# A hybrid diffusion block on one core: the router in a written order, the modulation product in four column groups, retention heads behind the last column blocks, the overflow branch moved, the last expert pair in full precision

## The chip, the core and the metric

The kernel runs on one core of a Trainium2 chip. The metric is the device time of one execution in microseconds (us). One core has a tensor engine (PE, with its weight loads shown apart as PEld), a vector engine (DVE), a scalar engine (ACT), GpSimd (POOL) and SyncE (SP), which here issues nearly all transfers. Each engine runs its own instructions in the order in which they stand in its queue.

## What is computed

One layer on 256 latent tokens and 256 context tokens of width 2048, all in fp32. Cut to what matters (plain_norm, silu and softmax as usual; S = 256, D = 2048):

```python
mod_x = split(silu(c) @ w_ada + b_ada, 6)          # six vectors of 2048 for the latent tokens
mod_c = split(silu(c_ctx) @ w_ada + b_ada, 6)      # the same for the context tokens
lat = modulate(x, mod_x[0], mod_x[1]) @ w_in       # 2048 -> qr kr vr gr (1024 each), cq 512, ckv 256, kpe 64
con = modulate(ctx, mod_c[0], mod_c[1]) @ w_in
s_fwd, s_bwd = context_retention_states(kr_c, vr_c)              # 8 heads of 128
ret = silu(gr) * plain_norm(bidirectional_retention(axial_rope(qr), axial_rope(kr), vr, s_fwd, s_bwd)) * gn_w
att = block_attention(mla_queries(cq), mla_keys_values(context and latent ckv, kpe))   # 8 heads
h = layer_norm(ALPHA * x + mod_x[2] * (concat(ret, att) @ w_o), ln1)
t = modulate(h, mod_x[3], mod_x[4])
g = argmax(t @ w_group + b_group)                                 # one of 4 groups
top2 = top_k((t @ w_route + b_route)[g], 2)                       # two of its 8 experts, weighted
y = sum over the 32 experts of gate * ((silu(t @ w_gate) * (t @ w_up)) @ w_down)       # 2048 -> 512 -> 2048
out = layer_norm(ALPHA * h + mod_x[5] * y, ln2)
```

## The kernel before, in words

The program is one straight line of stages. A scheduler that plans with its own costs places instructions of different statements between one another on each engine; what it decides is read from the order of the instructions.

**Modulation and input projection.** Of the six modulation vectors the first two (shift and scale ahead of the projection) are needed at once. gemv_plan makes them on TensorE: silu(c) and silu(c_ctx) are the stationary operand, a block of 128 rows by 32 columns, and the weights stream through. The block uses only 32 columns of the array, so the kernel has two 32-column groups run beside each other: a piece holds the columns of one of the two vectors (m) for some rows, and its even and odd row blocks go to the groups 2m and 2m+1 (L526). Weights come through `st`, four buffers of 1 MB that everything ahead of the experts streams through. The projection itself is done in six stages over blocks of 128 input rows: STAGES = 1, 1, 2, 4, 4 and 4 blocks. Within a stage the loop runs over chunks of w_in (a 1 MB chunk of four rows by 512 columns in the last three, ten chunks per stage, ci), loads one, splits it into a rounded part on ACT (L273) and a rest on DVE (L274), and multiplies three times (L594 to L596). Chunks that serve both streams fill four PSUM banks, those for latent tokens alone two. The modulation of stage k+1 is made during stage k: the loop hands out `todo`, the pieces of gemv_plan, over the chunks.

**The other four vectors** (m = 2 to 5) are made by ada_steps: one step takes 1 MB of w_ada, scaled and added up by two DVE instructions (L250) or by POOL. ADA_V says how many DVE steps stand behind which chunk, ADA_V_MLA behind each attention head. ada_finish (L210) brings the vectors 3 and 4 into a column form by 16 matmuls of one column (L215).

**Retention** runs in the last projection stage (stage 5). Behind chunk 3 the rotation of k goes to POOL (rope, L312 to L317), behind chunk 5 that of q to DVE, followed by all eight heads (ret_tables, ret_head: products with the context, scores L393, the mask on DVE L396 and L397, the result L402 and L404, L406 and L407 its statistics). Four chunks are left behind them: gates, cq and ckv/kpe.

**Attention, output projection, router.** The attention heads come next, then the output projection (L852 to L854) in four blocks n of 512 columns. Each block's end adds into h (L871, L872, statistics L873). The router's logits are computed from unnormalized h (router_part per half block, transposes L169, squares, L834 and L835) and corrected by mean and variance with many instructions of a few columns (L893 to L912), followed by maxima and one-hots (L944 to L954). The norm itself is `affine` (L181, L182), two DVE instructions per 128x512 piece, eight pieces; behind it each piece is normed again on ACT and split into a rounded part and a rest (nn). The counts of the selected tokens (L957 to L961) give each token its place, then tokens are gathered per expert by one-hot matmuls (L1049).

**Experts.** 32 experts in 16 pairs, 64 slots each. Every expert takes six chunks of 2 MB through a ring of six buffers, 192 chunks in all: gate and up (L1071), down (L1116). The result is scaled by the gate into a rounded part D (ACT, L1122) and a rest (DVE, L1123), and two matmuls per block (scatter, L1130) add it to the tokens, scaled by vector 5 and added to h (L1131, L1132). Gathering for the next two pairs happens between the down chunks of every odd pair. Only in pair 5 it doesn't: there overflow() (L1134 to L1138), a branch on whether an expert has more than 64 tokens, stands behind the downs and scatters, and eight gather steps stand behind it. The last pair's down chunks are ordered so that norm_part can make the final statistics block by block.

## Time and profile before

| what | value |
|---|---|
| median of three runs | 1685.78 us (1684.48 to 1687.98) |
| the profiled execution | 1686.18 us, of which its span is 1684.4 us |
| PE busy | 1521.6 us, 90% of the span |
| DVE, ACT, POOL busy | 919.9, 484.2, 105.9 us |
| read from memory | 575.81 MB; 343 GB/s over the span, written bytes included |

How to read it: shares over the whole span mix stages with different limits. The page gives the span in 40 slices of 42 us; a table by windows gives the busy time of every engine in each stage. In it, "(x231)" is a count of instructions, PEclk the granted clock as a share of full speed, and the last two columns are the DMA engines' busy share and what they moved. Where one line serves many places, groups are read by line and window.

### The profile page before, as it was taken

The page shows a single profiled execution, that of the slowest core. Times are in us where ns is not written, and L with a number is a line of the kernel's source. Part 1 is how long each engine was busy: PE and PEld are TensorE (multiplying, and loading weights), DVE is VectorE, ACT ScalarE, POOL GpSimd, SP SyncE. Part 2 cuts the span into 40 slices and gives each one's busy share as a digit, 9 for nine tenths or more (in the row PEclk, how much of TensorE's full clock was granted, in tenths as well). Part 3 has the DMA queues.
Part 4 walks back from the last instruction along what each step waited for, and adds up shares of the span by engine and source line. Part 5 has one row for each costly group of instructions (what it writes and reads, how often), then busy time and mean ns, then how long its engine had stood idle before and what let it go on. Part 6 is the DMA issues. An engine that isn't in the chain of part 4 may idle for free. (4 is left out here: it accounts for less than half of the span.)

```text
span 1684.4 us, 20454 instructions
## 1 busy us (share of the span) xinstructions
PE 1521.6 (90%) x8316; PEld 919.2 (55%) x8316; DVE 919.9 (55%) x1553; ACT 484.2 (29%) x913; POOL 105.9 (6%) x91
## 2 busy tenths in 40 slices
...
PEclk8999999998999999899999999999999999999997
...
GB/s 326 272 326 283 294 309 286 276 245 225 184 192 153 199 270 360 225 301 426 426 427 427 426 427 425 370 428 427 427 427 427 427 426 427 426 426 427 421 425 136
DMA packets 54226, 579.28 MB, mean 344 GB/s; under 512 B 6320, under 2 KB 6768, under 8 KB 8816
## 3 DMA queue, kind: packets, MB, share of 16 engines
...
q0 software_dynamic: 128, 0.03, 0.0%
HBM read 575.81 MB, written 2.10 MB: 343 GB/s over the span
## 5 line engine op out<-in xcount | busy, mean ns | idle before, releaser
L1071 PE MATMUL pA<-we,xg 128*64 128x512 f32 x2048 | 468.0, 602 | 12.8 <-DMA we<-in_wexp_dram 12.8
L1071 PEld LDWEIGHTS pA<-we,xg 128*64 128x64 f32 x2048 | 140.8, 138 | 281.2 <-issue 247.6
L1116 PE MATMUL pA<-we,hT 128*64 128x256 f32 x2048 | 232.7, 382 | 17.4 <-DMA we<-in_wexp_dram 16.1
L1123 DVE SCALAR_TENSOR_TENSOR D<-pA,gcol,D 64x256 fp32r<-64x256 f32 x256 | 123.5, 482 | 176.0 <-ACT D L1122 175.3
L273 ACT CAST whi<-st 128x1024 fp32r<-128x1024 f32 (+3 forms) x130 | 125.1, 965 | 282.5 <-PE pA L596 172.5
L1116 PEld LDWEIGHTS pA<-we,hT 128*64 128x64 f32 x2048 | 147.4, 137 | 92.2 <-ACT D L1122 8.7
L595 PE MATMUL pA<-wlo,xhi 128*128 128x512 f32 (+1 forms) x480 | 188.2, 392 | 10.5 <-DVE wlo L274 10.5
L594 PE MATMUL pA<-whi,xhi 128*128 128x512 f32 (+1 forms) x480 | 185.5, 394 | 3.3 <-ACT whi L273 3.1
L596 PE MATMUL pA<-whi,xlo 128*128 128x512 f32 (+1 forms) x480 | 185.8, 387 | 0.0
L250 DVE SCALAR_TENSOR_TENSOR ada_acc<-st,c,ada_acc 128x1024 f32<-128x1024 f32 x128 | 177.5, 1406 | 8.3 <-DMA st<-in_ada_dram 8.2
L274 DVE TENSOR_TENSOR wlo<-st,whi 128x1024 fp32r<-128x1024 f32 (+2 forms) x122 | 134.6, 1112 | 57.6 <-ACT whi L273 57.1
L1122 ACT ACTIVATE D<-pA,gcol 64x256 fp32r<-64x256 f32 x256 | 120.0, 469 | 156.7 <-PE pA L1116 87.5
L1074 ACT ACTIVATE hid<-pA 128x256 f32<-128x256 f32 x32 | 12.3, 383 | 493.5 <-PE pA L1071 493.5
L1075 DVE TENSOR_TENSOR hid<-pA,hid 128x256 f32<-128x256 f32 x32 | 13.5, 423 | 219.7 <-ACT hid L1074 219.7
L594 PEld LDWEIGHTS pA<-whi,xhi 128*128 128x128 f32 x480 | 90.5, 191 | 37.5 <-ACT whi L273 17.7
L595 PEld LDWEIGHTS pA<-wlo,xhi 128*128 128x128 f32 x480 | 91.9, 191 | 31.9 <-DVE wlo L274 14.5
L1058 DVE TENSOR_SCALAR xg<-pT,modt 128x256 f32<-128x256 f32 x64 | 34.8, 544 | 131.2 <-PE pA L1071 93.7
L1131 DVE TENSOR_TENSOR pA<-pA,ada_acc 128x512 f32<-128x512 f32 x128 | 83.5, 693 | 36.8 <-PE pA L1130 36.6
L596 PEld LDWEIGHTS pA<-whi,xlo 128*128 128x128 f32 x480 | 92.0, 192 | 16.3
L1049 PE MATMUL pT<-oh,nn 128*128 128x256 f32 x512 | 80.5, 303 | 9.1 <-DVEq L1136 5.8
L1049 PEld LDWEIGHTS pT<-oh,nn 128*128 128x128 f32 x512 | 68.3, 199 | 31.7 <-issue 20.5
L1132 DVE TENSOR_TENSOR h<-pA,h 128x512 f32<-128x512 f32 x128 | 82.6, 683 | 0.8
...
## 6 DMA issues: line engine op xcount, KB each, us to landing
we<-in_wexp_dram SPq DMA_DIRECT2D x190, 2048.0 KB, 21.8
...
```

What stands on the lines that cost most here:

```text
L250: V.scalar_tensor_tensor(accs[m][:, sl], w[:, sl], c2[:, k, 0:1], accs[m][:, sl], op0=OP.mult, op1=OP.add)
L273: A.copy(hi, src)
L274: (eng or V).tensor_tensor(lo, src, hi, op=OP.subtract)
L594: T.matmul(banks[t][:, :wd], xh[:, sl], hi[:, kk, :wd], start=fst, stop=False)
L595: T.matmul(banks[t][:, :wd], xh[:, sl], lo[:, kk, :wd], start=False, stop=False)
L596: T.matmul(banks[t][:, :wd], xl[:, sl], hi[:, kk, :wd], start=False, stop=lst)
L1049: T.matmul(p[:, 256 * j:256 * j + width], nnh[i % 2][:, i // 2, ks], oh[:, i // 2, :width], start=(i == 0), stop=(i == 3))
L1071: T.matmul(pg[64 * cg:64 * cg + 64], xg[:, k, c0:c0 + 64], c[:, kk, 512 * cg:512 * cg + 512], start=(k == 0), stop=(k == KB - 1))
L1116: T.matmul(pd[64 * cg:64 * cg + 64, :256], hT[:, f % 2, 64 * (f // 2):64 * (f // 2) + 64], c[:, f, 256 * cg:256 * cg + 256], start=(f == 0 ...
L1122: A.activation(hl[0][rows, sl], p, AF.Copy, scale=g)
L1123: V.scalar_tensor_tensor(hl[1][rows, sl], p, g, hl[0][rows, sl], op0=OP.mult, op1=OP.subtract)
L1131: V.tensor_tensor(p, p, mod5[:, sl], op=OP.mult)
```

## The change

Eight edits, in the order of the program:

1. **gemv pieces**: a piece now loads both vectors' columns, and for each row block runs m = 0 and m = 1 behind one another, so that four column groups are in use. GEMV_AT says behind which chunks of the ten-chunk stages the pieces stand. The order on PE of the start is written out (manual_schedule).
2. **Order of column blocks** in stages 1 to 4: blocks for both streams and blocks for latent tokens alone alternate.
3. **ada_finish**: four matmuls of 512 columns in four column groups, an ACT copy and four transposes in place of 16 matmuls of one column. **ada steps**: the sequence of DVE steps begins earlier (23 instead of 20 in stages 0 to 4, 10 instead of 14 in stage 5), attention has 17 instead of 14, and two steps of vector 5 fewer run in the output projection.
4. **Retention**: rope of k on DVE; heads 0 and 1 behind chunk 6, two more behind each of chunks 7, 8 and 9; a head's tables are made two heads ahead.
5. **router_consts**: four reductions, 1.4 us each, at four places of the output projection instead of one.
6. **Router**: from the last block on, the order of DVE, ACT and PE is written out. Of the eight norm instructions of each kind (L181 and L182 before, L913 and L917 after) three and two stand ahead of the selection, where square roots are awaited; the others stand behind it, in turn with the rests of nn. Small instructions of the two token tiles alternate.
7. **Overflow**: the branch stands behind gate and up of pair 5, ahead of its downs, and pair 5 gathers like the other odd pairs.
8. **Last pair**: D stays in fp32, the L1123 instructions fall away there, and the scatter is one fp32 matmul in place of two.

The places where instructions move, from the written order of the instructions. Names: pG is a bank of gemv_plan, pA a bank of a product, st a stream buffer, whi/wlo and xhi/xlo the rounded parts and rests of weights and inputs, lv, AM, Ssb and xq the values, masked scores, states and scaled queries of a retention head, qk its transposed queries and keys, ct the constants.

PE in stage 3, at one gemv piece, before:

```order
L594 MATMUL pA<-whi,xhi 128x512
L595 MATMUL pA<-wlo,xhi 128x512
L596 MATMUL pA<-whi,xlo 128x512
L526 MATMUL pG<-st,csil 32x512 x4
L594 MATMUL pA<-whi,xhi 128x512 x2
```

The same engine and stage after:

```order
L604 MATMUL pA<-wlo,xhi 128x512
L605 MATMUL pA<-whi,xlo 128x512
L535 MATMUL pG<-st,csil 32x512 x8
L603 MATMUL pA<-whi,xhi 128x512
L604 MATMUL pA<-wlo,xhi 128x512
```

Two pieces of four, 25 rows apart in the former order, have become one of eight; at some places of stages 3 and 4 it is split into one and seven.

PE in stage 5, from the middle of one retention head into the next, before:

```order
L402 MATMUL pA<-lv,AM 128x128
L404 MATMUL pA<-Ssb,xq 128x128 x2
L402 MATMUL pA<-lv,AM 128x128 x2
L404 MATMUL pA<-Ssb,xq 128x128 x2
L381 MATMUL pA<-vz,ck 128x256
L393 MATMUL pA<-qk 128x256 x2
L169 MATMUL pT<-ct,lq 128x128
L169 MATMUL pT<-ct,lk 128x128 x2
```

The same engine after, where a head ends behind which projection stands:

```order
L409 MATMUL pA<-lv,AM 128x128
L411 MATMUL pA<-Ssb,xq 128x128 x2
L409 MATMUL pA<-lv,AM 128x128 x2
L411 MATMUL pA<-Ssb,xq 128x128 x2
L604 MATMUL pA<-wlo,xhi 128x512
L605 MATMUL pA<-whi,xlo 128x512
L603 MATMUL pA<-whi,xhi 128x512
L604 MATMUL pA<-wlo,xhi 128x512
```

Between two pairs of heads now stand 20 to 24 projection matmuls; before, only the heads' own work stood there.

DVE in the router, from the correction of the logits to the first maxima, before:

```order
L182 SCALAR_TENSOR_TENSOR h<-h,hs,D_5453 128x512
L190 RECIPROCAL hs<-hs 128x2
L181 SCALAR_TENSOR_TENSOR h<-h,hs,D_5452 128x512
L909 TENSOR_TENSOR hs<-hs 128x2
L912 SCALAR_TENSOR_TENSOR L<-L,hs,rc 128x40 x2
L944 MAX gm<-L 128x8
L182 SCALAR_TENSOR_TENSOR h<-h,hs,D_5453 128x512
L945 MAX_INDEX gi<-gm,L 128x8
L944 MAX gm<-L 128x8
L181 SCALAR_TENSOR_TENSOR h<-h,hs,D_5452 128x512
```

The same engine after:

```order
L913 SCALAR_TENSOR_TENSOR h<-h,hs,D_5445 128x512
L957 RECIPROCAL hs<-hs 128x2
L958 TENSOR_TENSOR hs<-hs 128x2
L960 SCALAR_TENSOR_TENSOR L<-L,hs,rc 128x40 x2
L993 MAX gm<-L 128x8 x2
L994 MAX_INDEX gi<-gm,L 128x8
L1049 TENSOR_SCALAR w<-gm 128x1
L994 MAX_INDEX gi<-gm,L 128x8
L995 CAST gf<-gi 128x8
```

The 128x512 norm instructions that stood among the small ones are gone from there, but for the first.

The diff, cut to its core:

```diff
-ADA_V = [[0] * 10, [0] * 10, [0] * 5, [1] * 10, [1] * 10, [2] * 4 + [1] * 6]
+ADA_V = [[0] * 3, [1, 0, 0], [1, 1, 1, 0, 1], [1] * 7 + [0, 1, 1], [1] * 7 + [0, 1, 1], [1] * 10]
+
+GEMV_AT = (1, 3, 4, 5, 6)
...
         order = [2, 3, 4, 5, 0, 1, 9, 8, 6, 7]
+    elif si:
+        order = [0, 2, 1, 3, 6, 4, 7, 8, 5, 9]
     else:
...
-    ada_v = [(m, k) for m in (3, 4, 2) for k in range(KB)]
-    ada_g = [(5, k) for k in range(KB)]
+    ada_g = [(m, k) for m in (3, 4, 2, 5) for k in range(KB)]
+    ada_v = [ada_g.pop(0) for _ in range(50)]
...
             p = bankT()
-            for k in range(KB):
-                T.matmul(p[:, k:k + 1], acc[:, 128 * k:128 * k + 128], ones[:, 0:1], start=True, stop=True)
-            if m == 4:
-                V.tensor_scalar(modt[:, 1], p[:, :KB], 1.0, None, op0=OP.add)
-            else:
-                V.tensor_copy(modt[:, 0], p[:, :KB])
+            for g in range(4):
+                T.matmul(p[32 * g:32 * g + 32], ones[:, 0:32], acc[:, 512 * g:512 * g + 512], start=True, stop=True)
+            row = sa.tile([128, 2048], F32, name="st", tag="st")[:, :512]
+            A.copy(row, p)
+            p = bankT()
+            for j in range(4):
+                transpose(p[:, 128 * j:128 * j + 128], row[:, 128 * j:128 * j + 128])
+            V.tensor_scalar(modt[:, m - 3].rearrange("p (g j) -> p g j", g=4),
+                            p.rearrange("p (j g r) -> p g j r", j=4, g=4)[:, :, :, 0], float(m - 3), None, op0=OP.add)
...
-        def piece(j, m):
+        def piece(j):
...
-                c = stream(dram2(a["ada01"], base + (m * nch + j) * 128 * per * w, 128, per * w), per * w)
+                c = [stream(dram2(a["ada01"], base + (m * nch + j) * 128 * per * w, 128, per * w), per * w)
+                     for m in range(2)]
                 for kk in range(per):
                     k = j * per + kk
-                    g = 2 * m + (k % 2)
-                    T.matmul(p[32 * g:32 * g + 32, :w], csil[:, k], c[:, kk * w:kk * w + w],
-                             start=(k < 2), stop=(k >= KB - 2))
+                    for m in range(2):
+                        g = 2 * m + (k % 2)
+                        T.matmul(p[32 * g:32 * g + 32, :w], csil[:, k], c[m][:, kk * w:kk * w + w],
+                                 start=(k < 2), stop=(k >= KB - 2))
...
         for j in range(nch):
-            pieces.append(piece(j, 0))
-            pieces.append(piece(j, 1))
+            pieces.append(piece(j))
...
+            if nchunk == 10:
+                n = GEMV_AT.count(ci)
...
-                            rope(pl["k"][:, t, 512 * j:512 * j + 512], t, "ck", "sk", 4, 64, R["rt"], G)
+                            rope(pl["k"][:, t, 512 * j:512 * j + 512], t, "ck", "sk", 4, 64, R["rt"])
                 elif ci == 5:
                     for t in range(2):
                         for j in range(2):
                             rope(pl["q"][:, t, 512 * j:512 * j + 512], t, "cq", "sq", 4, 64, R["rt"])
-                    for h in range(H):
+                    for h in range(2):
                         ret_tables(h)
+                if ci > 5:
+                    for h in range(2 * ci - 12, 2 * ci - 10):
                         ret_head(h)
-                elif ci == LAT:
+                        if h < H - 2:
+                            ret_tables(h + 2)
...
-    ada_steps(48, 0)
+    ada_steps(len(ada_v), 0)
...
-        for i, v in enumerate((pr[0], pr[2], pr[1], wrm)):
-            V.tensor_reduce(rc[:, i], v.rearrange("p k n -> p n k"), axis=AX.X, op=OP.add)
-        return bias
+        return bias, (pr[0], pr[2], pr[1], wrm)
+
+    def router_const(i, v):
+        V.tensor_reduce(rc[:, i], v.rearrange("p k n -> p n k"), axis=AX.X, op=OP.add)
...
+                if 1 <= 4 * n + k4 <= 4:
+                    router_const(4 * n + k4 - 1, rparts[4 * n + k4 - 1])
...
-                V.bn_stats(st1[:, t, n], h[:, t, sl])
+                if n < 3:
+                    V.bn_stats(st1[:, t, n], h[:, t, sl])
+        pinned = tc.manual_schedule(engines={V.engine, A.engine, T.engine})
+        pinned.__enter__()
+        flipped = [router_flip(3, half) for half in range(2)]
         for half in range(2):
-            router_part(3, half)
+            router_rest(3, half, flipped[half])
+        for t in range(2):
+            V.bn_stats(st1[:, t, 3], h[:, t, 1536:2048])
         for t in range(2):
             V.bn_aggr(hs[:, t, 0:2], st1[:, t].rearrange("p n s -> p (n s)"))
-        rstd_of(hs[:, :, 1:2], hs[:, :, 1:2])
+        A.activation(hs[:, :, 1:2], hs[:, :, 1:2], AF.Sqrt, bias=eps)
+
+        def norm_a(t, c):
+            cs = slice(512 * c, 512 * c + 512)
+            V.scalar_tensor_tensor(h[:, t, cs], h[:, t, cs], hs[:, t, 0:1], lnw[:, cs], op0=OP.subtract, op1=OP.mult)
+
+        def norm_b(t, c):
+            cs = slice(512 * c, 512 * c + 512)
+            V.scalar_tensor_tensor(h[:, t, cs], h[:, t, cs], hs[:, t, 1:2], lnb[:, cs], op0=OP.mult, op1=OP.add)
+
         V.tensor_scalar(hs[:, :, 2:3], hs[:, :, 0:1], -1.0, None, op0=OP.mult)
+        norm_a(0, 0)
+        norm_a(1, 0)
+        V.reciprocal(hs[:, :, 1:2], hs[:, :, 1:2])
+        norm_b(0, 0)
+        norm_b(1, 0)
         lT = wo.tile([128, 2, S], F32, name="lT")
         A.copy(lT[:40, 0], rcp[:40, :S])
-        V.tensor_copy(lT[:40, 1], rcp[64:104, :S])
+        A.copy(lT[:40, 1], rcp[64:104, :S])
...
-        rstd_of(hs[:, :, 4:5], x0)
+        A.activation(hs[:, :, 4:5], x0, AF.Sqrt, bias=eps)
+        for t in range(2):
+            V.scalar_tensor_tensor(L[:, t], rc[:, 1], hs[:, t, 3:4], L[:, t], op0=OP.mult, op1=OP.add)
+        norm_a(0, 1)
+        V.reciprocal(hs[:, :, 4:5], hs[:, :, 4:5])
...
-    def norms():
-
-        for c0 in range(0, D, 512):
-            cs = slice(c0, c0 + 512)
-            for t in range(2):
-                affine(V, h[:, t, cs], hs[:, t, 0:1], hs[:, t, 1:2], lnw[:, cs], lnb[:, cs], None)
-                f = nnfp.tile([128, 512], F32, name="nnf")
-                A.activation(f, h[:, t, cs], AF.Identity, bias=hs[:, t, 5:6], scale=hs[:, t, 4:5])
-                hi_lo(nnh[0][:, t, cs], nnh[1][:, t, cs], f)
+    def normed(t, c):
+
+        cs = slice(512 * c, 512 * c + 512)
+        f = nnfp.tile([128, 512], F32, name="nnf")
+        A.activation(f, h[:, t, cs], AF.Identity, bias=hs[:, t, 5:6], scale=hs[:, t, 4:5])
+        return A.copy(nnh[0][:, t, cs], f), f
+
+    def normed_lo(t, c, f):
+        cs = slice(512 * c, 512 * c + 512)
+        V.tensor_tensor(nnh[1][:, t, cs], f, nnh[0][:, t, cs], op=OP.subtract)
...
+    fs = [normed(t, 0)[1] for t in range(2)]
+    for f in (lambda t: V.max(gm[:, t], L[:, t, 0:8]),
...
+              lambda t: V.scalar_tensor_tensor(sel[:, t], iota[:, 0:E], ef[:, t, 1:2], o1[:, t], op0=OP.is_equal, op1=OP.add)):
+        for t in range(2):
+            f(t)
+
+    p = bankT()
+    T.matmul(p[:, 0:32], C("ut"), sel[:, 0], start=True, stop=True)
+    T.matmul(p[:, 32:64], ones, sel[:, 0], start=True, stop=False)
+    T.matmul(p[:, 32:64], C("ut"), sel[:, 1], start=False, stop=True)
+    norm_a(1, 1)
     for t in range(2):
...
+        V.scalar_tensor_tensor(rk[:, t], p[:, 32 * t:32 * t + 32], 1.0, sel[:, t], op0=OP.add, op1=OP.mult)
+        normed_lo(t, 0, fs[t])
...
-    norms()
+    for c in range(1, 4):
+        for t in range(2):
+            if c > 1:
+                norm_a(t, c)
+            norm_b(t, c)
+            done, f = normed(t, c)
+            normed_lo(t, c, f)
...
+    pinned.__exit__(None, None, None)
...
+        D1 = dp.tile([128, 4, 512], F32, name="D0")
+        return [[D1[:, n]] for n in range(4)]
...
-            V.scalar_tensor_tensor(hl[1][rows, sl], p, g, hl[0][rows, sl], op0=OP.mult, op1=OP.subtract)
+            if len(hl) > 1:
+                V.scalar_tensor_tensor(hl[1][rows, sl], p, g, hl[0][rows, sl], op0=OP.mult, op1=OP.subtract)
...
-            for j in range(2):
-                T.matmul(p, sT[:K, t, :], hl[j][:K], start=(j == 0), stop=(j == 1))
+            if len(hl) == 1:
+                T.matmul(p, sT[:K, t, :].bitcast(F32), hl[0][:K], start=True, stop=True)
+            else:
+                for j in range(2):
+                    T.matmul(p, sT[:K, t, :], hl[j][:K], start=(j == 0), stop=(j == 1))
...
-            router_weights()
+            with tc.issue_after(done.ins):
+                router_weights()
         hid1 = gate_up(xg, 128 * pq + 64, src[1], second)
         hT, sT, gcol = box["hT"], box["sT"], box["g"]
-        hl = new_D()
-        gather = pq and not final and pr != 5
+        if pr == 5:
+            overflow()
+        hl = new_D_whole() if final else new_D()
+        gather = pq and not final
...
-        if pr == 5:
-            for n in range(4):
-                scatter(hl[n], sT, 128, n)
-            hl = None
-            overflow()
-            oh = new_places(pr // 2 + 1)
-            xg = new_xg()
-            for k2 in range(0, KB, 2):
-                gather_two(xg, k2, oh, 256)
```

## Rows read from the trace of the kernel before

**Rows 1.** The page: clock and memory by 40 slices, and the issues of expert weights.

```profile
PEclk8999999998999999899999999999999999999997
GB/s 326 272 326 283 294 309 286 276 245 225 184 192 153 199 270 360 225 301 426 426 427 427 426 427 425 370 428 427 427 427 427 427 426 427 426 426 427 421 425 136
...
we<-in_wexp_dram SPq DMA_DIRECT2D x190, 2048.0 KB, 21.8
```

**Rows 2.** Table by windows: stages 3 and 4; 5 in three parts; attention to 1640.

```profile
143.04:239.60 96.56, 96.56 (x451) 70.21 (x450) 66.80 (x79) 27.20 (x37) 0.00 (x0) 1.00 0.75 290
239.60:338.40 98.80, 98.80 (x482) 73.68 (x481) 68.16 (x81) 27.21 (x37) 2.30 (x2) 1.00 0.77 294
338.40:400.00 61.60, 55.77 (x229) 44.41 (x228) 57.84 (x78) 18.61 (x27) 30.34 (x28) 0.94 0.67 243
400.00:457.00 57.00, 45.17 (x260) 39.60 (x259) 44.33 (x93) 35.48 (x87) 32.88 (x30) 0.88 0.52 186
457.00:487.00 30.00, 27.76 (x154) 23.34 (x153) 27.77 (x65) 22.75 (x52) 2.45 (x1) 1.00 0.61 218
487.00:580.00 93.00, 85.75 (x482) 70.09 (x481) 80.77 (x139) 53.83 (x108) 19.36 (x8) 0.98 0.45 165
580.00:691.00 111.00, 106.17 (x475) 81.01 (x475) 80.03 (x81) 39.51 (x45) 7.08 (x8) 0.98 0.77 294
691.00:742.00 51.00, 37.18 (x185) 20.17 (x185) 32.50 (x108) 27.77 (x45) 0.00 (x0) 0.83 0.60 237
742.00:1640.00 898.00, 824.76 (x4806) 399.25 (x4802) 321.50 (x611) 172.02 (x366) 0.00 (x0) 0.99 1.00 423
```

**Rows 3.** Timeline of PE at gemv pieces: start, length, instruction, count.

```profile
118.66 1.94 PE L526 MATMUL pG<-st,csil 128*32 128x512 f32 x16
...
172.90 1.91 PE L526 MATMUL pG<-st,csil 128*32 128x512 f32 x8
```

**Rows 4.** Groups of PE by line and form: busy us, mean ns, idle before.

```profile
L526 PE MATMUL pG<-st,csil 128*32 128x512 f32 x192 | 39.3, 599 | 0.0
...
L526 PE MATMUL pG<-st,csil 128*32 128x256 f32 x64 | 9.7, 386 | 0.0
...
L215 PE MATMUL pT<-ones,ada_acc 128*128 128x1 f32 x64 | 8.0, 258 | 1.0 <-ACT qk L388 1.0
```

**Rows 5.** Groups of DVE from 348 to 380, while POOL rotates k.

```profile
L250 DVE SCALAR_TENSOR_TENSOR ada_acc<-st,c,ada_acc 128x1024 f32<-128x1024 f32 x8 | 13.7, 1718 | 0.0
...
L347 DVE TENSOR_SCALAR ze<-r_lg,ct 128x8 f32<-128x8 f32 x4 | 2.8, 764 | 0.0
```

**Rows 6.** Groups of DVE: ada steps from 200 to 330, rotation of q from 400.

```profile
L250 DVE SCALAR_TENSOR_TENSOR ada_acc<-st,c,ada_acc 128x1024 f32<-128x1024 f32 x29 | 35.8, 1279 | 0.0
...
L316 DVE TENSOR_TENSOR lq<-lq,rp 128x256 f32<-128x256 f32 x4 | 1.7, 418 | 0.0
```

**Rows 7.** Waits of PE by what ended them, from 400 to 460: us, times, longest.

```profile
PE pA L402 <- DVE AM L396: 2.7, 2, 1.4
```

**Rows 8.** The same from 580 to 691.

```profile
PE pA L853 <- DVE wlo L274: 4.8, 3, 4.1
```

**Rows 9.** The router: waits of PE from 690; DVE's norm instructions from 690.9.

```profile
PE pA L957 <- DVE w L992: 12.6, 1, 12.6
...
L182 DVE SCALAR_TENSOR_TENSOR h<-h,hs,D 128x512 f32<-128x512 f32 x8 | 6.0, 748 | 0.0
L181 DVE SCALAR_TENSOR_TENSOR h<-h,hs,D 128x512 f32<-128x512 f32 x8 | 5.7, 735 | 0.0
```

**Rows 10.** Timeline of PE behind the overflow branch: the first gather steps.

```profile
1072.02 4.79 PE L1049 MATMUL pT<-oh,nn 128*128 128x256 f32 x24 [5.76 <-DVEq L1136]
```

**Rows 11.** Groups from 1640 to the end, and an fp32 product of 512 columns.

```profile
L1123 DVE SCALAR_TENSOR_TENSOR D<-pA,gcol,D 64x256 fp32r<-64x256 f32 x16 | 7.7, 482 | 5.4 <-ACT D L1122 5.2
...
L1130 PE MATMUL pA<-D,sT 128*128 128x512 f32 x16 | 5.1, 429 | 2.5 <-ACT D L1122 2.5
...
L661 PE MATMUL pA<-st,cqall 128*128 128x512 f32 x16 | 7.2, 593 | 0.0
```

52 lines of the change are left out of this document (25 added, 27 removed).

## Prediction

> **What bounds the kernel now.** I read the page's 40 slices first, then a table by windows, then groups and waits of the windows that the change touches. The slices show two halves [rows 1]: from about 720 us on memory delivers 426 to 428 GB/s, before that mostly 150 to 330. The table by windows gives the reason. In the expert stretch 742 to 1640 the memory moved 423 GB/s with the DMA engines 100% busy [rows 2], and 190 loads of 2 MB plus the 4 half ones stand behind it [rows 1]: 2097 KB at 427 GB/s are 4.9 us each, so some 183 loads behind 742 take 897 us, and nothing on an engine shortens them. What precedes that stretch moves its start, and so the end, one for one; inside it only a hole in the stream counts; behind it only the tail. Stages 3 and 4 are bound by PE: 96.56 of 96.56 and 98.80 of 98.80 us busy, with the DMA engines at 0.75 and 0.77 and DVE at 0.69 [rows 2]. Stage 5 is mixed: 338 to 400 has DVE at 57.84 of 61.60 and POOL at 30.34, 400 to 457 (the heads) has no engine above 45.17 of 57.00 at a clock of 0.88, and 457 to 487 PE and DVE both 93% [rows 2]. Attention is close to both PE and DVE (85.75 and 80.77 of 93). The router stretch 691 to 742 is latency: PE 37.18 of 51, clock 0.83.
>
> **The change, part by part.** The sums are made against the profiled execution, 1686.18 us with its span of 1684.4; the median of the runs, 1685.78, is 0.4 less, and that is taken off at the end.
>
> *Gemv, 14 us.* One piece of 8 instructions of 512 columns takes 1.91 us; where two pieces happened to stand beside each other, 16 take 1.94 [rows 3]. So four groups run in the time of two, and pairing saves 1.9 us per pair. The 192 instructions of 512 columns [rows 4] are 24 pieces, 12 pairs, of which two ran together already. Each of the other ten saves 1.9, or 1.5 where the new order splits it into one and seven and one group's share of 0.4 is lost: 10 x 1.5 = 15. The 256-column ones (64, 9.7 us busy [rows 4]) and those of stage 1 halve at best for about 4 more; that makes 19 at the top. I take 14, since each piece now needs two loads at once from four buffers: 2.1 MB are 4.9 us at 427 GB/s, and the memory's slack in these stages is a quarter. Low end 0, if every gain turns into waiting for the second load (one load of 1 MB is 2.45 us, more than the 1.9 saved). The order of column blocks changes no work and is costed at nothing, under PE's cover; without it, it is a part of the same waits.
>
> The Trainium skill, page "TensorE: Matmul & The Clock Gate", section "Measured speedup vs the span model", has four row tiles at 3.07 times and three column tiles at 2.38 times, not four and three. By it four groups would cost 1.3 of one matmul and this term would be about 10 at most. The row above shows no such loss, 1.94 against 1.91 us, and the measurement decides.
>
> *ada_finish, 2 us in stage 4.* Two finishes of 32 one-column instructions (16 matmuls) cost 8.0 us [rows 4], 4.0 each. Four concurrent matmuls of 512 columns are about half a piece of eight, 1 us, and four transposes about another 1. The ACT copy between them has projection work behind which to hide. Bounds 0 and 3. The second finish lies among the heads and is counted there.
>
> *Retention and k's rotation, 15 us.* The stretch 338.4 to 487 takes 148.6 us with 128.7 us of PE work and 129.9 us of DVE work [rows 2], some of both inflated. On DVE: while POOL rotates k, an ada step's instruction takes 1718 ns, against 1279 in stages 3 and 4, and an eight-column one 764 ns [rows 5, 6]. With POOL gone, 8 x 0.44 + 4 x 0.6 and similar on some 20 small ones come to 8 to 10 us less; the rotation itself adds 24 x 0.418 = 10.0 us, and four ada steps fewer take off 4 x 2 x 1.28 = 10.2. DVE then has some 120 to 122 us. On PE: half a clock step in the heads' stretch (0.88 of full) is some 6 us of the 45.17; without it, and without 2 of the ada_finish, 121 us. So the stage cannot fall under about 121 us (gain 27). What fills the heads' waiting are the 120 projection matmuls x 0.23 = 27 us that stood behind them; what stays are waits inside a pair, since PE's queue is in order: two heads per pair, each with a turn over ACT, PE and the DVE mask. I leave 1.5 us of them per head, 12 in all: 121 + 12 = 133, gain 15. Bounds 0 (no overlap) and 27.
>
> *Attention, -2 us.* Three more ada steps are 3 x 2 x 1.28 = 7.7 us of DVE work in a window with 12.2 us of DVE idle [rows 2]. Bounds 0 (all in the idle time) and -8 (DVE ends last). I take -2, nearer to the idle time since PE too has 7 us free there.
>
> *Output projection, 3.5 us.* PE waited 4.1 us at one place for a weight rest on DVE [rows 8]; the four reductions of 1.4 us stood there at once. Spread over four chunks each is shorter than DVE's slack per chunk (80 of 111 us busy, so 1.9 us on each of 16 chunks [rows 2]). Bounds 0 and 4.8.
>
> *Router, 5 us.* From the last output matmul to the first count on PE 21 us pass, of them 12.6 in one wait [rows 9], with DVE at work nearly throughout. In that time it ran all 16 norm instructions, 6.0 + 5.7 us [rows 9], and three rests of nn (0.69 each). Ahead of the selection five of the norms now remain. That takes 11 x 0.73 + 2.1 = 10 us off DVE's queue. Against that the small instructions, some 50, lose their cover: dependent ones then cost 0.15 instead of 0.07 us, 4 us in all. That leaves 6 us. What is late next is gathering: the norms return between the gather steps, 10 us more of DVE work in the last 30 us of the stretch, where DVE was busy for 32.5 - 21 = 11.5. I take 1 off. Bounds -3 (gathers wait for the written order on ACT and DVE) and 10.
>
> *Overflow, 5.5 us.* At the branch PE waits 5.76 us and then does gathers with no expert work beside them, 4.8 us for the first three steps [rows 10]; the page's slice there fell to 370 GB/s [rows 1]. A slice of 42.1 us at 57 GB/s less is 5.6 us of lost transfer. After the change DVE reaches the branch with nothing queued, and gathers lie under the downs as in the other odd pairs. What waits at the new branch: SP's further issues, but up to five loads (24 us) are under way there. Bounds 0 and 5.7.
>
> *Tail, 1.5 us.* Of the 16 L1123 (482 ns [rows 11]) only those that stand between the last loads and the end count, some 9 or 4.3 us of DVE. Against it the scatter: two rounded matmuls of 512 columns took 16 x 0.32 = 5.1 us in all [rows 11], an fp32 one is two instructions of 0.45 in sequence (7.2 us for 16 [rows 11]), so 2 more on PE. Bounds -1 and 4.
>
> Sum: 14 + 2 + 15 - 2 + 3.5 + 5 + 5.5 + 1.5 = 44.5. 1686.2 - 44.5 = 1641.7, less 0.4 for the median: **1641 us**.
>
> **The rivals.**
>
> *Loads end last in stages 1 to 4.* If pairs of loads wait, the gemv term is 0 to 3: 1652 to 1655. For it speaks that a piece takes two of four buffers; against it that the DMA engines have a quarter of these stages free [rows 2].
>
> *Heads gain nothing, and DVE ends last in attention.* The retention term is 0 to 3, attention -5 to -8: 1641 + 13 + 5 = 1659, up to 1662, and to 1668 with half of the first rival. For it: DVE at 57.84 of 61.60 and 80.77 of 93 [rows 2]. Against it: 27 us of projection without dependence on the heads.
>
> *Heads hold the projection (slower).* PE's queue is in order. If in every head three turns over DVE (two masks and the statistics) each wait behind an ada step's two instructions (2 x 1.46 us, their mean beside the heads), a head costs 8.8 us more, eight heads 70, and the weights behind them come no sooner: 1641 + 70 - some cover of 10 to 20 = 1691 to 1701. It decides from 5.6 us per head. Against it: with all eight heads behind one another and the same ada steps beside them, PE's waits for the first mask were 2.7 us in total [rows 7].
>
> *The change doesn't do what it says.* Matmuls of the two vectors run one after the other after all, and every gain ahead of the experts is taken up by the earliest loads of weights: within 0.2% of 1685.8. The first expert loads are in place long before they are used, which speaks against it.
>
> **How the numbers follow.** Forecast 0.60 (1622 to 1654), loads 0.14, heads without gain 0.13, no change 0.05, slower 0.08. The range 1620 to 1668 takes in the forecast with its bounds and the first two rivals, 0.87 less their tails. A measurement of this kernel can tell 0.2%, 3.4 us, from no change. Faster 0.60 + 0.14 + 0.13 = 0.87, same 0.05, slower 0.08.
>
> **What would show it.** In the profile after: gemv groups of eight at about 1.9 us; some 5 us off stage 3 and 7 off stage 4, or, if loads end last, PE's waits for the buffers of the modulation weights there. Stage 5 near 133 us and PE clock 1.00 in it. Attention near 95. The first count on PE some 15 us behind the last output matmul, and the first expert result 26 to 29 us behind that. No slice of the expert stretch under 420 GB/s. DVE without L1123 behind the last load. Wrong it would be if the expert stretch's start does not come 35 to 45 us earlier, or if the stream, once started, shows new holes.

## The result and the profile after

The changed kernel takes 1666.41 us (median of four runs, 1664.87 to 1668.01), the kernel before 1685.64; the ratio is 0.9884, with a 95% interval of 0.9867 to 0.9901. It is faster by 19 us, where 44.5 had been forecast: the right side, inside the range, and less than half the size. Repeated on another chip it took 1667.57 against 1684.59, 0.9891 [0.9863, 0.9919]. The ratios leave out two executions, 7089 and 2551 us, of the ten of a combination shown further below, one in each of its two studies; no other kernel had such ones, no trace caught one, and their cause is open.

Both traces cut at the same events show where the time went. A time in the table runs from the first instruction of one stage to that of the next (from the trace); "steady stream" is the landing of the 41st expert load. The instants before and after are in brackets. The two profiled executions lie 21.3 us apart, 2 more than the medians.

| part | before, us | after, us | change | forecast |
|---|---|---|---|---|
| start, stage 0 | 54.2 | 54.6 | +0.3 | 0 |
| stage 1 | 35.7 | 32.3 | -3.4 | |
| stage 2 | 53.1 | 57.2 | +4.1 | |
| stage 3 | 96.6 | 92.8 | -3.8 | |
| stage 4 | 98.8 | 92.8 | -6.0 | -16 for stages 1 to 4 with the finish |
| stage 5 to the first attention scores (510.3, 488.5) | 171.9 | 158.8 | -13.1 | -15 |
| to the output projection | 71.9 | 75.9 | +4.0 | +2 |
| output projection | 108.9 | 109.1 | +0.2 | -3.5 |
| router and first experts, to the steady stream (902.3, 882.2) | 211.2 | 208.7 | -2.5 | -5 |
| over pair 5, to the 91st load (1154.7, 1134.1) | 252.4 | 251.9 | -0.5 | -5.5 |
| to the 191st load | 491.4 | 492.3 | +0.9 | 0 |
| tail | 38.3 | 36.7 | -1.6 | -1.5 |

The table by windows after (columns as in [rows 2]): stage 2, 3, 4, stage 5 to its last projection matmul, the passage to the first attention scores, attention, output projection. Stage 2 and the passage of the kernel before, which [rows 2] lacks, follow it.

```profile
86.90:144.10 57.20, 53.09 (x265) 37.91 (x263) 40.63 (x58) 16.74 (x27) 0.00 (x0) 0.94 0.79 311
144.10:236.90 92.80, 92.77 (x450) 69.38 (x450) 65.79 (x78) 27.10 (x37) 0.00 (x0) 1.00 0.74 284
236.90:329.70 92.80, 91.94 (x463) 69.98 (x462) 63.18 (x77) 27.54 (x38) 2.29 (x2) 1.00 0.73 291
329.70:446.70 117.00, 109.13 (x562) 90.57 (x562) 107.10 (x226) 66.24 (x143) 36.77 (x30) 1.00 0.56 209
446.70:488.50 41.80, 32.88 (x161) 25.15 (x159) 36.89 (x62) 26.68 (x52) 10.14 (x7) 0.84 0.46 175
488.50:564.40 75.90, 69.00 (x389) 58.79 (x387) 66.39 (x109) 40.59 (x83) 15.48 (x6) 0.96 0.60 222
564.40:673.50 109.10, 103.91 (x466) 77.96 (x464) 82.62 (x83) 38.30 (x43) 7.08 (x8) 1.00 0.80 307
```

```profile
89.95:143.04 53.09, 51.98 (x262) 36.60 (x261) 38.60 (x54) 17.05 (x27) 0.00 (x0) 1.00 0.80 313
487.10:510.30 23.20, 19.79 (x105) 13.83 (x104) 22.91 (x38) 14.44 (x28) 6.42 (x3) 1.00 0.34 125
```

Against [rows 2] the reader is to see three things: stages 3 and 4 still run with PE busy throughout, so the time that they gave up is PE work; stage 2 has the only clock below 1.00 among the stages 1 to 4 (0.94, before 1.00); and in stage 5 the last projection matmul comes 40 us earlier (446.7, before 487.1) at full clock, but a passage of 41.8 us at clock 0.84 follows it, where 23 us at full clock had lain before.

The product for the modulation did shrink as summed. These groups of the changed kernel answer to [rows 4]:

```profile
L535 PE MATMUL pG<-st,csil 128*32 128x512 f32 x192 | 28.4, 599 | 0.0
L535 PE MATMUL pG<-st,csil 128*32 128x256 f32 x64 | 6.7, 389 | 0.0
L535 PE MATMUL pG<-st,csil 128*32 128x128 f32 x128 | 6.6, 348 | 14.3 <-DMA st<-in_ada_dram 14.3
L219 PE MATMUL pT<-ada_acc,ones 128*32 128x512 f32 x16 | 3.1, 596 | 2.4 <-ACT qk L395 2.4
```

28.4 stands for 39.3 us and 6.7 for 9.7; with the 128-column form (10.1 before) 17.4 us of PE time are gone. In the timeline of PE an unsplit piece of two vectors is 16 instructions in 1.92 us, as long as 8 of one vector were in [rows 3]; a split one costs 1.05 us more, where the prediction had 0.4:

```profile
203.44 1.92 PE L535 MATMUL pG<-st,csil 128*32 128x512 f32 x16
...
188.92 1.05 PE L535 MATMUL pG<-st,csil 128*32 128x512 f32 x2
...
190.49 1.92 PE L535 MATMUL pG<-st,csil 128*32 128x512 f32 x14
```

The loss weighed in the prediction by the Trainium skill (page "TensorE: Matmul & The Clock Gate", section "Measured speedup vs the span model") does not show here either, from two column groups to four: they take the same time, 1.92 and 1.91 us.

The slices of memory still have one dip in the expert stretch, 374 GB/s where the page before had 370 [rows 1], though the branch now stands elsewhere:

```profile
GB/s 324 293 340 274 350 187 307 307 243 154 245 176 236 210 312 368 211 357 426 427 426 427 427 426 374 426 426 427 427 427 426 426 427 426 427 427 426 426 426 135
```

### The profile page after: what moved, and what is told of

The parts are those of the page before. It is cut to its first block, busy times and chain, and to the rows that moved or that the text cites. A ratio compares the mean times of both kernels' runs of the same rounds, so it can differ in the third digit from the quotient of the medians.

```text
span 1663.1 us, 20375 instructions
## 1 busy us (share of the span) xinstructions
PE 1511.1 (91%) x8276; PEld 909.4 (55%) x8276; DVE 912.9 (55%) x1560; ACT 486.5 (29%) x917; POOL 83.3 (5%) x67
## 5 line engine op out<-in xcount | busy, mean ns | idle before, releaser
L1188 DVE SCALAR_TENSOR_TENSOR D<-pA,gcol,D 64x256 fp32r<-64x256 f32 x240 | 115.8, 483 | 174.5 <-ACT D L1186 174.0
L257 DVE SCALAR_TENSOR_TENSOR ada_acc<-st,c,ada_acc 128x1024 f32<-128x1024 f32 x128 | 173.3, 1370 | 6.5 <-DMA st<-in_ada_dram 6.5
L1186 ACT ACTIVATE D<-pA,gcol 64x256 fp32r<-64x256 f32 (+1 forms) x256 | 120.0, 469 | 158.2 <-PE pA L1180 96.5
L605 PEld LDWEIGHTS pA<-whi,xlo 128*128 128x128 f32 x480 | 91.5, 191 | 16.5 <-DVE xlo L566 0.2
```

The lines of the kernel that those rows point to most:

```text
L257: V.scalar_tensor_tensor(accs[m][:, sl], w[:, sl], c2[:, k, 0:1], accs[m][:, sl], op0=OP.mult, op1=OP.add)
L605: T.matmul(banks[t][:, :wd], xl[:, sl], hi[:, kk, :wd], start=False, stop=lst)
L1186: A.activation(hl[0][rows, sl], p, AF.Copy, scale=g)
L1188: V.scalar_tensor_tensor(hl[1][rows, sl], p, g, hl[0][rows, sl], op0=OP.mult, op1=OP.subtract)
```

## The experiments

Medians are of runs on different chips; each is compared by its ratio to the kernel before on its own chip. The intervals reach 0.2% to 0.3% (4 to 5 us) to either side, so a step of 5 us between two runs is likely and not certain; stages are compared by the traces, one execution of each kernel.

**The pieces alone, in the kernel before.** Only gemv_plan changed:

```diff
-        def piece(j, m):
+        def piece(j):
...
-                    T.matmul(p[32 * g:32 * g + 32, :w], csil[:, k], c[:, kk * w:kk * w + w],
...
+                    for m in range(2):
+                        g = 2 * m + (k % 2)
+                        T.matmul(p[32 * g:32 * g + 32, :w], csil[:, k], c[m][:, kk * w:kk * w + w],
...
```

> The kernel before with the gemv pieces alone changed: each piece loads both vectors and uses four column groups; the order of column blocks, the ada steps and all else stay. If four groups halve the product's time, as the prediction had it, stages 1 to 4 end about 14 us earlier and the whole takes 1672 (1668 to 1676). If the two loads per piece take the four stream buffers from the projection's weights, as the trace of the changed kernel shows in stage 2 (no load of projection weights issued from 102 to 110 us, PE short of work until 119), the gain is 3 to 8 us, 1678 to 1683, and PE's waits for split weights in stages 1 to 4 are longer than before.

1707.4 us, ratio 1.0122 [1.0096, 1.0148]: not a smaller gain but 21 us lost. By windows of stages 2, 3 and 4:

```profile
88.10:149.30 61.20, 55.89 (x263) 39.41 (x263) 39.93 (x57) 17.06 (x27) 0.00 (x0) 0.92 0.74 282
149.30:246.10 96.80, 94.05 (x451) 70.42 (x449) 69.01 (x79) 26.83 (x37) 0.00 (x0) 0.98 0.79 302
246.10:348.30 102.20, 99.34 (x483) 75.45 (x481) 68.03 (x82) 26.85 (x37) 2.29 (x2) 0.95 0.75 284
```

and its waits of PE over stages 1 to 4 (us, times, longest):

```profile
PE pA L595 <- ACT whi L273: 4.9, 7, 1.7
PE pA L596 <- DVE wlo L274: 2.6, 4, 0.8
PE pG L537 <- ACT row L534: 2.2, 3, 0.7
```

PE now waits for split projection weights, seven times in place of once, and its clock falls. The pieces take PE work away and starve the rest. Stages 1 to 4 take 8 us longer by this (292.2 us, before 284.2). Two more are lost ahead of them, and some 11 behind them, where nothing was edited; the trace leaves open why.

**The changed kernel with the former order of column blocks.** The prediction costed this edit at nothing.

```diff
-    elif si:
-        order = [0, 2, 1, 3, 6, 4, 7, 8, 5, 9]
```

> The changed kernel with the column blocks of stages 1 to 4 in their former order. The prediction costed this order at nothing. The pieces alone, in the former order, made stages 3 and 4 no shorter (96.8 and 102.2 us against 96.6 and 98.8), with PE waiting for split weights and the clock at 0.95 to 0.98; in the changed kernel they take 92.8 each. If the alternating order is what keeps PE supplied while a piece holds two of the four stream buffers, stages 2 to 4 take 6 to 15 us longer without it: 1671 to 1682. If GEMV_AT (fixed places of the pieces) does that, nothing changes: 1664 to 1668.

1676.95 us, ratio 0.9942 [0.9921, 0.9962], against 0.9884 [0.9867, 0.9901] with the alternating order: it is worth about 10 us. By the first matmul of each stage, its stages 2 to 4 take 61.2, 91.4 and 97.7 us instead of 57.2, 92.8 and 92.8: the loss lies in stages 2 and 4, and stage 3 does without the order. Over stages 1 to 4 that is 7 us; the rest comes behind them. PE waits for the splits again:

```profile
PE pA L601 <- ACT whi L278: 7.0, 8, 2.7
PE pA L602 <- DVE wlo L279: 2.1, 2, 1.5
PE pG L533 <- DMA st<-in_ada_dram: 2.1, 2, 1.1
```

And ACT, which makes the splits, waits longer for projection weights to land; in these four stages of this run, then of the changed kernel:

```profile
ACT whi L278 <- DMA st<-in_win_dram: 59.7, 7, 10.0
```

```profile
ACT whi L280 <- DMA st<-in_win_dram: 35.7, 4, 10.7
```

A block for both streams gives PE 10.9 us of work (48 matmuls of 0.227 us), one for latent tokens alone 5.45, from the same 1 MB. That a block for both behind every short one bridges the time in which a piece holds two of the four buffers is the likely reason; what the order is worth without the pieces was not run.

**The changed kernel with one-vector pieces.** The places are kept, two where one stood with pieces in two groups as before.

```diff
-GEMV_AT = (1, 3, 4, 5, 6)
+GEMV_AT = (1, 1, 3, 3, 4, 4, 5, 5, 6)
...
-            pieces.append(piece(j))
+            pieces.append(piece(j, 0))
+            pieces.append(piece(j, 1))
```

> The changed kernel with the gemv pieces as they were: one vector and two column groups each, two pieces where one stood. If the pairs saved what the prediction summed (about 2 us of PE per pair, 14 in all), stages 1 to 4 take that longer and the whole takes 1676 to 1681. If pairing the loads costs as much as pairing the matmuls saves, as the run with pieces alone suggests (21 us slower than before, 8 of them in stage 2), the whole takes 1660 to 1668 and stage 2 (87 to 144 us in the changed kernel) gets shorter by 3 to 8 us.

1674.6 us, 0.9916 [0.9892, 0.9940], 5 to 8 us slower than the changed kernel. But this run does not undo what it meant to: its trace shows all pairs but one of stages 3 and 4 side by side, 16 instructions in 1.94 us, and stages 3 and 4 at 91.5 and 92.6 us, as fast as in the changed kernel. So it can't say what four groups are worth. What makes four groups run is that two pieces stand beside each other, whoever wrote them so. The difference lies in stage 1 (36.4 instead of 32.3 us) and behind stage 4.

**Stage 2: ada steps taken out.** In the changed kernel SP's issues and PE at the end of stage 2 read:

```profile
91.83 0.38 SPq L146 DMA_DIRECT2D st<-in_win_dram  x1
92.31 10.85 SPq L146 DMA_DIRECT2D st<-in_ada_dram  x5
110.78 2.73 SPq L146 DMA_DIRECT2D st<-in_win_dram  x4
```

```profile
108.82 3.79 PE L535 MATMUL pG<-st,csil 128*32 128x512 f32 x32
113.33 1.05 PE L544 MATMUL pG<-ct,row 128*128 128x4 f32 x8 [0.72 <-ACT row L541]
115.25 0.90 PE L173 MATMUL pT<-ct,xn 128*128 128x128 f32 x4 [0.87 <-ACT xf L564]
117.12 1.14 PE L173 MATMUL pT<-ct,xn 128*128 128x128 f32 x4 [0.97 <-ACT xf L564]
119.12 2.16 PE L603 MATMUL pA<-whi,xhi 128*128 128x512 f32 x4 [0.86 <-ACT whi L280]
```

Five loads of modulation weights in a row hold all buffers, no projection weights are issued between 91.8 and 110.8 us, and PE, left with the chain from the vectors to the next stage's inputs, falls to half clock from about 116 to 123 us (granted clock 0.60 from 115 to 120, 0.71 from 120 to 125).

```diff
-ADA_V = [[0] * 3, [1, 0, 0], [1, 1, 1, 0, 1], [1] * 7 + [0, 1, 1], [1] * 7 + [0, 1, 1], [1] * 10]
+ADA_V = [[0] * 3, [1, 0, 0], [0, 0, 0, 0, 1], [1] * 10, [1] * 10, [1] * 10]
...
-    ada_v = [ada_g.pop(0) for _ in range(50)]
+    ada_v = [ada_g.pop(0) for _ in range(48)]
```

> The changed kernel with three ada steps of stage 2 taken out, one more in stages 3 and 4 each, and 48 steps on DVE's list. In the changed kernel all four stream buffers hold modulation weights from 102 to 111 us, so projection weights are loaded late and PE idles and falls to half clock from 113 to 123. If buffers are the cause, three loads fewer in stage 2 end it 3 to 6 us earlier (stage 3 begins at 138 to 141 instead of 144) and the whole takes 1657 to 1662, the 4.6 us of the run with steps moved earlier being a part of it. If the two loads of a gemv piece alone suffice to starve it, stage 3 begins at 143 to 145 and the whole takes 1662 to 1665.

1679.1 us, 0.9941 [0.9919, 0.9964]. Stage 2 takes 59.3 us, not less: the four loads of two pieces follow one another just so, and again no projection weights are issued between 92.8 and 111.8 us. That the ada steps hold the buffers falls. This run lost another 12 us in attention, where 34 instead of 29 of the ada instructions ran on DVE (104.6 us busy against 91.2).

**Stage 2: its pieces spread.**

```diff
+            if nchunk == 5:
+                n = (2, 1, 2, 0, 0)[ci]
```

> The changed kernel with the gemv pieces of stage 2 handed out as 2, 1, 1 and the end instead of 2, 2 and the end. In the changed kernel the third and fourth piece's four loads follow one another on SyncE's queue (100.5 to 103 us) and fill all four stream buffers; the next projection load is issued at 110.8. Taking ada steps out did not help. If two pieces in a row are the cause, stage 3 begins 3 to 7 us earlier (137 to 141 instead of 144) and the clock stays full there; the whole takes 1660 to 1664. If the planner brings the pieces together again, or one piece's pair of loads is enough, nothing changes: 1664 to 1668.

1662.4 us, 0.9844 [0.9824, 0.9864]. Stage 2 takes 54.4 us instead of 57.2, so two pieces in a row were two thirds of the 4.1 us lost there; the rest stays. How much of it reaches the end is less clear: the profiled execution was this kernel's slowest, 1664.6 us, and in it the lead is gone by the first attention scores (488.5 us in both traces).

**Without the overflow branch**, so that the work for experts with more than 64 tokens is left out, once in the changed kernel and once in the kernel before (where the eight open gather steps stay). Changed kernel first:

```diff
-        if pr == 5:
-            overflow()
```

> The changed kernel without the overflow branch (the work for experts with more than 64 tokens is left out). In the changed kernel SyncE stands at the branch from 997.7 to 1021.9 us, until its own last load has landed, and the next two loads land 8.6 and 6.3 us behind the former one instead of 4.9. If this draining is what a branch costs wherever it stands, the kernel takes 5 us less, 1661.3, and no slice of the expert stretch is under 420 GB/s. If the hole came from the engines' arrival at the new place, or is made up for by buffers, the gain is under 2 us: 1664.5 to 1666.5.

> The kernel before without its overflow branch (the work for experts with more than 64 tokens is left out); the eight gather steps of pair 5 stay where they stand, behind its scatters. If the hole in the stream of loads is the draining of SyncE's own loads at the branch, as in the changed kernel, it is gone here too although the gathers still lie open: about 5 us less, 1680 to 1682, and no two expert loads land more than 5.5 us apart behind 742. If the open gathers and DVE's late arrival made the hole, as the prediction had it, under 2 us come back: 1684 to 1686.

1663.0 us, 0.9854 [0.9832, 0.9876], and 1678.3 us, 0.9941 [0.9918, 0.9964]. From the first down matmul to the end the changed kernel takes 927.5 us and 922.8 without the branch; the kernel before 928.6 and 923.3. The branch cost 5.3 us at its old place and 4.7 at its new one. The ratio of the second run says 10 us; in its trace 4.2 of them are stage 0 (50.0 us at full clock, in the trace of before 54.2 at 0.91), where nothing was edited. Windows of the changed kernel around its branch, then without it:

```profile
990.00:1010.00 20.00, 18.76 (x80) 6.58 (x78) 6.62 (x14) 0.76 (x2) 0.00 (x0) 0.91 1.01 427
1010.00:1035.00 25.00, 19.09 (x100) 9.50 (x96) 3.42 (x8) 3.77 (x8) 0.00 (x0) 0.86 0.83 337
```

```profile
990.00:1010.00 20.00, 18.75 (x89) 8.04 (x89) 9.66 (x19) 0.76 (x2) 0.00 (x0) 1.00 1.00 425
1010.00:1035.00 25.00, 22.60 (x141) 11.48 (x139) 4.88 (x10) 5.62 (x12) 0.00 (x0) 1.00 1.01 426
```

The same view of the kernel before, with its branch and, second, without:

```profile
1060.00:1085.00 25.00, 17.08 (x90) 12.41 (x88) 14.84 (x25) 4.57 (x9) 0.00 (x0) 0.86 0.88 358
```

```profile
1060.00:1085.00 25.00, 21.79 (x104) 8.89 (x102) 12.15 (x21) 2.09 (x5) 0.00 (x0) 0.93 1.00 426
```

At the branch SP stops issuing until the last load it has issued has landed: in the kernel before from 1045.9 us, its last load landing at 1070.55 and the next issue at 1070.72, ahead of DVE's arrival at 1071.6; in the changed kernel from 997.7 us, landing at 1021.02, next issue at 1021.99. With nothing under way the next load needs 8.9 and 7.6 us. That the late DVE and the open gathers made the hole falls. What SP does there, before and after:

```profile
L1136 SPq EVENT_SEMAPHORE  x8: 17/17/17, 1046.4 to 1070.6; - x8
L1136 SPq COMPARE_BRANCH  x1: 50/50/50, 1045.9 to 1045.9; - x1
```

```profile
L1204 SPq EVENT_SEMAPHORE  x8: 17/17/17, 1016.2 to 1021.8; - x8
L1204 SPq COMPARE_BRANCH  x1: 50/50/50, 997.7 to 997.7; - x1
```

The branch itself takes 50 ns. What holds SP are eight instructions on semaphores that stand with it in SP's queue; in the kernel before the last four of them start within 0.1 us behind one landing each. So the wait is in the program, put there with the branch; no run has a branch without them, or one in which SP takes no part.

**Ada steps earlier, and heads earlier.** Two runs on the end of retention and on attention, in the changed kernel:

```diff
-... [1] * 7 + [0, 1, 1], [1] * 7 + [0, 1, 1], [1] * 10]
+... [1] * 10, [1] * 10, [1] * 10]
...
-    ada_v = [ada_g.pop(0) for _ in range(50)]
+    ada_v = [ada_g.pop(0) for _ in range(48)]
```

> The changed kernel with one ada step more in each of stages 3 and 4 and two fewer taken by DVE's list in all: 35 steps stand ahead of attention instead of 33, 13 are left for it instead of 17, and the output projection has 16 again. Attention's part took 8.8 us more than before the change. If DVE's ada steps end last there (32 such instructions of 1.58 us between 447 and 564, 22 before), 8 instructions fewer give 5 to 9 us: 1658 to 1661. If what was lost is the end of retention, which now stands between the last projection block and attention, with PE waiting for ACT, POOL and DVE in turn and at half clock, the gain is 0 to 3 us: 1663.5 to 1667.

```diff
-                    for h in range(2 * ci - 12, 2 * ci - 10):
+                    for h in {6: (0, 1), 7: (2, 3, 4), 8: (5, 6, 7)}.get(ci, ()):
```

> The changed kernel with retention heads 2 to 4 behind chunk 7 and 5 to 7 behind chunk 8, none behind the last chunk, so that the last block stands behind the last head and the second half of norm and output may run beside it. If the end of retention is what attention lost, 4 to 9 us come back: 1657 to 1662. If ada steps on DVE are the loss, nothing comes back, or three heads per block wait longer for each other: 1665 to 1670.

1661.8 us, 0.9851 [0.9829, 0.9874], and 1662.8 us, 0.9853 [0.9831, 0.9875]. Neither reason wins. The first run's attention did not get shorter (104.5 us from its first product to the output projection, 103.3 in the changed kernel); its gain lies ahead and behind. The second reached the output projection 5 us earlier, but spent 113.4 us there instead of 109.1. What PE waits for in the passage of the changed kernel is a chain over DVE and ACT:

```profile
457.02 0.82 PE L173 MATMUL pT<-ct,lq 128*128 128x128 f32 x4 [2.56 <-DVE lq L436]
469.04 0.43 PE L173 MATMUL pT<-ct,lq 128*128 128x128 f32 x2 [0.86 <-DVE lq L436]
470.75 1.32 PE L173 MATMUL pT<-ct,lq 128*128 128x128 f32 x6 [1.28 <-DVE lq L436]
475.26 0.79 PE L296 MATMUL pA<-kv,whi 128*128 128x512 f32 x1 [3.20 <-ACT kv L280]
```

The first of these waits stands behind a DVE instruction that took 2.71 us, while POOL split weights (454.1 to 459.2 us); the same one took 0.69 with POOL idle:

```profile
454.25 2.71 DVE L436 TENSOR_TENSOR lq<-lq,lg 128x512 f32<-128x512 f32 x1
...
468.20 0.69 DVE L436 TENSOR_TENSOR lq<-lq,lg 128x512 f32<-128x512 f32 x1 [1.71 <-ACT lq L428]
```

**The heads' edit alone**, with k's rotation on DVE, in the kernel before: the hunks of the diff on rope and on ci 5 and above, and nothing else.

```diff
-                    for h in range(H):
+                    for h in range(2):
                         ret_tables(h)
+                if ci > 5:
+                    for h in range(2 * ci - 12, 2 * ci - 10):
                         ret_head(h)
```

> The kernel before with k's rotation on DVE and the heads in pairs behind the last four blocks, nothing else changed. The prediction gave this 12 us together with the rotation. By the changed kernel's trace the last projection ends 31 us earlier within stage 5, but the heads' end and the second half of retention's norm then stand open ahead of attention, and 13 us are left at the first attention scores, less 4 within attention. If that is due to this edit, the whole takes 1674 to 1679. If it needs the other edits (fewer ada steps in stage 5, the cheaper finish of the modulation vectors), 1680 to 1686.

1676.3 us, 0.9938 [0.9918, 0.9958]: 10 us, whole by itself. Its output projection begins 9.7 us earlier counted from the start of stage 5.

**The former finish of the modulation vectors** in the changed kernel, and later in the combination.

```diff
-            for g in range(4):
-                T.matmul(p[32 * g:32 * g + 32], ones[:, 0:32], acc[:, 512 * g:512 * g + 512], start=True, stop=True)
...
+            for k in range(KB):
+                T.matmul(p[:, k:k + 1], acc[:, 128 * k:128 * k + 128], ones[:, 0:1], start=True, stop=True)
```

> The changed kernel with the former ada_finish (16 matmuls of one column, one DVE instruction). By the prediction stage 4 takes 2 us longer and the heads 2 to 3: 1669 to 1671. If the new finish's own chain (product, copy on ACT, four transposes) costs as much where it stands, nothing changes: 1665 to 1668.

1661.5 us, 0.9859 [0.9834, 0.9885]. Stage 4 is 1 us longer, as forecast in sign, but the passage from the last projection to the first attention scores is 2.5 us shorter (39.3), and so is attention (73.4).

**The router's norms one piece ahead.** The rest of nn is issued behind the next piece's norm:

```diff
+            if late_lo:
+                normed_lo(*late_lo)
+            late_lo = t, c, f
-            normed_lo(t, c, f)
```

> The changed kernel with one change in the router's written order: each rest of nn stands one piece later on DVE, behind the next piece's two norm instructions. In the changed kernel a piece takes 3.9 us (norm on DVE 1.5, two casts on ACT 1.43, rest on DVE 0.69, each waiting for the one ahead), six pieces 23 us, and the first gate and up end 28.8 us behind the first gather against 26.6 before. If this chain ends last there, a piece falls to about 2.3 us, the first gate and up end 4 to 8 us earlier and the whole takes 1659 to 1663. If PE's own work and the memory (ring of six loads, next free slot) end last, 0 to 2 us: 1664.5 to 1667.

1666.6 us, 0.9872 [0.9850, 0.9894]. The waits of DVE between 690 and 717 us (us, times, longest), in the changed kernel and in this run:

```profile
DVE nn L982 <- ACT nn L978: 6.0, 5, 1.5
```

```profile
DVE nn L982 <- ACT nn L978: 0.9, 1, 0.9
```

The chain is broken as meant, and the first gate and up end 27.1 instead of 28.8 us behind the first gather. But of the 28.8 us PE was busy for 27.0, so no more than 1.8 us was there to gain; the time of the whole moves by less than its interval.

**The reductions later.**

```diff
-                if 1 <= 4 * n + k4 <= 4:
-                    router_const(4 * n + k4 - 1, rparts[4 * n + k4 - 1])
+                if 3 <= 4 * n + k4 <= 6:
+                    router_const(4 * n + k4 - 3, rparts[4 * n + k4 - 3])
```

> The changed kernel with the four reductions of the router's constants behind chunks 3 to 6 of the output projection instead of 1 to 4. In the changed kernel PE still waits 3.1 us at 581.8 for a weight rest on DVE, which stands behind a reduction that itself waits 1.8 us for POOL's product (POOL is done at 580.7). If that order is the cause, both waits of 3.1 and 0.6 us vanish and the whole takes 1662 to 1664. If the output projection is bound by the loads instead (307 GB/s there, and expert loads between), under 1.5 us: 1665 to 1667.

1666.9 us, 0.9871 [0.9838, 0.9904]: nothing. The changed kernel's DVE shows the fault:

```profile
578.70 1.39 DVE L827 TENSOR_REDUCE rc<-st 128x40 f32<-128x640 f32 x1 [1.78 <-POOL st L821]
580.01 1.73 DVE L281 TENSOR_TENSOR wlo<-st,whi 128x1024 fp32r<-128x1024 f32 x1
581.67 1.40 DVE L827 TENSOR_REDUCE rc<-st 128x40 f32<-128x640 f32 x1
```

A reduction waits 1.78 us for POOL, and the weight rest behind it makes PE wait 3.1. In this run the same reduction again waits 1.78 us ahead of the same rest and PE again 3.13: the planner moved the reductions up although the code has them two chunks later.

**Together.** Ada steps earlier, pieces of stage 2 spread, heads earlier, norms one ahead, and the reductions held until POOL's last product; then once more, and with the former finish; beside them the changed kernel again. Of the edits only the last has not stood above:

```diff
-                    router_const(4 * n + k4 - 1, rparts[4 * n + k4 - 1])
+                    with tc.issue_after(rbox["prod"].ins):
+                        router_const(4 * n + k4 - 1, rparts[4 * n + k4 - 1])
```

> The changed kernel with all of these: ada steps earlier (35 ahead of attention), gemv pieces of stage 2 as 2, 1, 1, heads as 2, 3 and 3 behind chunks 6 to 8, rests of nn one piece later, and the reductions of the router's constants only once POOL has made the last product. Taken singly the first three gave 4.6, an unknown and 3.6 us, the fourth about 1. If they add up, 1652 to 1658. If the second and third meet the same limit (the memory in the output projection, DVE in attention), 1659 to 1663.

> The five changes together once more, with five rounds: in the first try three executions took 1657.1 to 1659.7 us and one 7089. If they hold, the median is 1656 to 1660 and all executions lie within 6 us; a long one again would mean that the kernel itself can stall.

> The combination with the former ada_finish. Alone, the former finish made the changed kernel 5 us faster, its gain lying between the last projection and the first work of attention (the new finish's product, copy and transposes stand in the retention heads' queue). If that adds to the combination, whose heads end a block earlier, 1650 to 1654. If the combination's earlier heads have already taken the finish off the path, 1656 to 1659.

> The changed kernel unaltered, for a comparison on one chip and to see whether it too has executions far longer than the rest, as two of the combination's ten. By its four runs 1664 to 1668.

The combination: 0.9826 [0.9803, 0.9850] and 0.9824 [0.9803, 0.9845], 1656.5 us in the second study, 10 us under the changed kernel. Taken singly, four of its edits come to some 20 us by their ratios, so they don't add up. The fifth did not do what it was meant to: a reduction still waits 1.78 us for POOL, and PE 3.2 us for the weight rest behind it (first study, 550 to 670 us):

```profile
PE pA L881 <- DVE wlo L281: 3.9, 3, 3.2
```

With the former finish the combination loses: 0.9861 [0.9831, 0.9890], where the changed kernel had 0.9891 [0.9863, 0.9919] on the same chip. Its stage 4 takes 96.6 us, the combination's 92.6. The finish that cost the changed kernel some 4 us seems to gain the combination about as much; the intervals overlap in both cases.

## Why the prediction came out wrong

Of the 23 us that are missing between the two profiled executions, the gemv term with the finish has 7, the overflow 5, the output projection 3.7, the router 2.5, heads and attention 2 each. By the prediction's own sign, too, it is wrong: the steady stream starts 20 us earlier and not 35 to 45.

*Gemv: right mechanism, wrong balance.* Four groups run in the time of two, and PE lost 17.4 us of work against 19 at the top of the sum. (Its parts were off both ways: the 512-column pieces gave 10.9 us and not 15, since in the trace of before four pairs and not two already stand side by side, near 105, 119, 150 and 245 us; the shorter forms gave 6.5 and not 4.) The step that failed is that the order of column blocks "is costed at nothing, under PE's cover". There was no such cover: a piece takes two of four buffers. Without the order the pieces lose 21 us in the kernel before (8 of them in stages 1 to 4) and the changed kernel 10 (7). Even with it, stage 2 lost 4.1 us. The rival of loads that end last was thus true in stage 2 and held off by another edit in stage 4; it had been weighed as one case or the other for all stages. The term came to 9 with the finish, not 16.

*Overflow: the cause was wrong.* The sum took the 5.6 us hole from the page rightly and put it down to DVE's late arrival and the open gathers. That "up to five loads (24 us) are under way" was meant as cover; it is what SP waits for. SP's row at the branch stood in the trace of before: it reached the branch 26 us ahead of DVE and went on before DVE had come. The hole moved with the branch and cost 4.7 us in place of 5.3: 0.5 us gained, not 5.5.

*Output projection: 0 instead of 3.5.* The step "each is shorter than DVE's slack per chunk" took the places in the code for the places on the engine, and left out that a reduction on DVE waits for POOL. PE's one wait of 4.1 us [rows 8] became one of 3.1, and the stretch got no shorter.

*Router: 2.5 instead of 5.* The counts come 14.4 us behind the last output matmul, 6.5 us sooner than before, where 6 had been worked out. The terms of what is late next were short: the way from the counts to the first gather grew from 1.5 to 2.8 us, the gathers with gate and up from 26.6 to 28.8 (1 us had been taken off), and from there to the steady stream 0.5 more was lost.

*Heads and attention: the size held, in part by luck.* -13.1 for -15 and +4.0 for +2, both inside their bounds. The sum had 133 us up to the last projection matmul and called 121 the least; it took 117, since the end of the last heads now lies behind it. There 18.6 us came back as the passage with nothing to fill it, for which the prediction had no term. The two errors nearly cancel. The tail held, -1.6 for -1.5. The finish, summed at 2 us and 2 more among the heads, was not a gain in this kernel; its worth seems to change sign with what stands beside it.

In all, work that is taken away came out near its sums (17.4 us of PE for 19, 6.5 us up to the counts for 6). The terms that failed concern what an edit does to others: buffers, a queue's wait, a planner that packs again. Seven terms of one sign were added with each one's likely value, and beside the gemv term (14 of 19) and the router's gathers (1 us) none was charged for what it shares with others.
